# Loading the first tile of a streamed dot product in four strided transfers

## The chip, the cores and the metric

The kernel runs on one core of one Trainium2 chip. The metric is the time of one execution on the device, in microseconds (us); lower is better. Times below are medians of several executions. Executions in the normal (fast) state lie within 1 us of their kernel's median, most of them within 0.4; the few executions in a slower state are named where they occur and are not used in comparisons. The span in a profile (first to last instruction) is some 1.8 us shorter than the time of the same execution.

## The reference

x is 8 x 2048 x 4096 float32, 268 MB, and w has 4096 numbers. Each row of x is multiplied with w; along each of the 8 sequences the running maximum of these dot products is taken; a position counts as a record where it reaches that maximum; the output is the running count of records.

```
proj = (x @ w).squeeze(-1)
cm = np.maximum.accumulate(proj, axis=1)
is_record = (proj >= cm).astype(np.float32)
return np.cumsum(is_record, axis=1).astype(np.float32)
```

All the bytes are in x, and each is used once.

## The kernel before

x streams from HBM (the chip's main memory) into three large buffers in SBUF (the memory on the core, 128 rows called partitions). A tile is one sequence's 512 positions: 128 partitions, each with r = 4 neighbouring positions, that is 64 KB per partition and 8 MB in all. (The last group has r = 3, and 128 positions at the end of each sequence are loaded in smaller pieces.) All loads of x are issued by the sync engine's queue in one long list; a load waits only until its buffer is free.

```
for g in range(NG):
    r = RS[g]
    for t in range(B):
        i = SY.dma_start(
            out=at(g, t)[:, : r * D],
            in_=x[B - 1 - t, STARTS[g] : STARTS[g] + r * P, :].rearrange(
                "(p r) d -> p (r d)", r=r
            ),
        ).then_inc(xs[t], 16)
        u, n = user_before(g, t)
        if n:
            i._wait_ge(*(free(u, n)))
        ...
```

The compute of a tile starts when the whole tile has landed: the vector engine (DVE) takes 2816 of the 4096 columns of each row as a fused dot product, the POOL engine multiplies the other 1280, and ACT sums POOL's products. Both wait on the tile's semaphore:

```
def group_dots(r, g=0):
    for t in range(B):
        b, xb = B - 1 - t, at(g, t)
        for j in range(r):
            i = dot(xb[:, j * D : j * D + VC], w_v[:, :VC], ...)
            if j == 0:
                i._wait_ge(xs[t], 16)
        i.then_inc(fr[t], 1)
...
def group_products(r, g=0):
    ...
            i = G.tensor_mul(out=xl, in0=xl, in1=w_sb).then_inc(pl, 1)
            if j == 0:
                i._wait_ge(xs[t], 16)
```

After each group the tensor engine transposes the sums and the vector engine scans them. w is spread to all partitions at the start, beside the load of the first tile.

Of the kernel before, what the change touches and what calls it, by code (L numbers as in the profile page):

```python
# [20 lines left out]
def kernel(  # L21
# [16 lines left out]
    P = 128  # L38
    B, S, D = x.shape
# [8 lines left out]
    STARTS = [sum(RS[:g]) * P for g in range(NG)]  # L48
# [19 lines left out]
    def rows_of(m):  # L68
        return m * H % B, m * H // B * Q
# [41 lines left out]
    def sem(name):  # L111
        return tc.alloc_semaphore(f"{name}_{next(ns)}")
# [1 line left out]
    xs = [sem("xs") for _ in range(B)]  # L114
    fr = [sem("fr") for _ in range(B)]
    xq = [sem("xq") for _ in TILES]
    ws, bw, wc, cs, od, oe, psr, pd, pl, go, sd, pa, con, fo, ms, p7, mg, pg, ml = (
        sem(n) for n in "ws bw wc cs od oe psr pd pl go sd pa con fo ms p7 mg pg ml".split()
    )

    V, A, G, T, SY = nc.vector, nc.scalar, nc.gpsimd, nc.tensor, nc.sync
# [28 lines left out]
    def at(g, t):  # L150
        return xbuf[(t if g < NL else t + NS - 1) % NS]

    def user_before(g, t):
        if t >= NS:
            return t - NS, g + 1
        if g == NL:
            return B - NS + t, g
        return max(u for u in range(B) if u % NS == t), g

    def free(u, n):  # L160
        return (p7, n) if u == B - 1 else (fr[u], 2 * n)

    with tc.tile_critical(no_gpsimd_drain=True):

        for g in range(NG):
            r = RS[g]
            for t in range(B):
                i = SY.dma_start(
                    out=at(g, t)[:, : r * D],
                    in_=x[B - 1 - t, STARTS[g] : STARTS[g] + r * P, :].rearrange(  # L170
                        "(p r) d -> p (r d)", r=r
                    ),
                ).then_inc(xs[t], 16)
                u, n = user_before(g, t)
                if n:
                    i._wait_ge(*(free(u, n)))
                if g == t == 0:
                    A.dma_start(
                        out=w_row, in_=w.rearrange("(k c) one -> k (c one)", k=NW)
                    ).then_inc(ws, 16)  # L180
                if t == 4 and g:
                    SY.dma_start(
                        out=out[:, STARTS[g - 1] : STARTS[g]], in_=cnt
                    )._wait_ge(cs, g + 1).then_inc(od, 16)
# [9 lines left out]
        for i, (m, c0, c1, _, _) in enumerate(TILES):  # L194
            u, xb = slot(m)
            d = SY.dma_start(  # L196
                out=xb[:, c0:c1],
                in_=x[
                    rows_of(m)[0] : rows_of(m)[0] + H,
                    S0 + rows_of(m)[1] : S0 + rows_of(m)[1] + Q, c0:c1,  # L200
                ].rearrange("b i d -> i b d"),
            ).then_inc(xq[i], 16)
# [7 lines left out]
            out=identity, in_=identity, compare_op=ALU.not_equal, fill=1.0,  # L210
# [10 lines left out]
        for n, k in enumerate(order):  # L221
# [3 lines left out]
                out=dst, lhsT=identity[:NW, k : k + 1].to_broadcast([NW, P]),  # L225
# [13 lines left out]
            out=by_b, in_=identity.rearrange("p (i b) -> p b i", b=H),  # L239
# [3 lines left out]
            out=by_i, in_=identity.rearrange("p (i b) -> p i b", b=H), op=ALU.add,  # L243
# [4 lines left out]
        def group_scans(r=R):  # L248
            n = r * P
            scans(cm[:, :n], cnt[:, :n], ps[:B, :n], cm[:, N - 1 :], cnt[:, N - 1 :])  # L250
# [5 lines that stand above are left out]
                    i = dot(  # L256
                        xb[:, j * D : j * D + VC], w_v[:, :VC],
                        sum_v[:, j * B + b : j * B + b + 1],
                    )
                    if j == 0:  # L260
                        i._wait_ge(xs[t], 16)
                i.then_inc(fr[t], 1)

        with V.Fori(0, NL):
            group_scans()
            V.sem_inc(psr, -3)
            group_dots(R)
# [4 lines left out]
# [3 lines that stand above are left out]
                    xl = at(g, t)[:, j * D + VC : (j + 1) * D]  # L275
                    i = G.tensor_mul(out=xl, in0=xl, in1=w_sb).then_inc(pl, 1)  # L276
                    if j == 0:
                        i._wait_ge(xs[t], 16)

        G.wait_ge(wc, 3)  # L280
        with G.Fori(0, NL):
            group_products(R)
# [87 lines left out]
        for m in range(B - 2):  # L370
            k = m // 2
            v, p = acc_v[:, m : m + 1], acc_p[:, m : m + 1]
# [16 lines left out]
        for i in range(B - 2, len(TILES)):  # L389
            n = i - (B - 2)  # L390
            m, p = TILES[i][0], TILES[i][4]
            z = m - (B - 2)
            v, dp = part_v[:, n : n + 1], part_p[:, n : n + 1]
# [53 lines left out]
```

## Time and profile before

| | before |
|---|---|
| time, median of the first 3 runs | 630.17 us |
| span of the profiled run | 629.3 us |
| x by the stream's rate, 268.44 MB at 433 GB/s | 620 us |
| first dot product on x | 22.80 us |

The page's DMA rows and the rates by stretch are in the prediction. Two more views matter for what follows. The first is the rate in the two halves of the first tile's load (columns as in the prediction: start:end, length, five engines, clock, DMA share, GB/s; a packet counts in the stretch where it starts, so short stretches are rough and a DMA share can exceed 1):

```profile
2.00:12.00 10.00, 9.38 (x11) 3.81 (x12) 0.57 (x2) 1.87 (x2) 0.00 (x0) 1.00 1.01 413
12.00:22.00 10.00, 4.63 (x6) 1.33 (x4) 3.58 (x4) 1.47 (x2) 0.00 (x0) 1.00 1.00 433
```

The second is the start of the first dot product in the vector engine's timeline (start us, duration, what, the idle time before it and what ended that):

```profile
22.80 3.09 DVE L124 CUSTOM_DVE_ANT_0 xall<-xall,w_v 128x2816 f32<-128x2816 f32 x1 [0.67 <-DMA xall<-in_x_dram]
```

The first tile streams at once at nearly the full rate, and the vector engine finishes its setup only 0.67 us before the tile is there.

Below, "row" means the data of one partition of a tile, which the trace records as one DMA packet of 65,536 bytes. The records have no engine and no address. In order of their start they fall into rounds of 16, because 16 streams run side by side; each stream is taken to be one DMA engine, which so moves eight rows of a tile. "Row one" is the first such round.

### The profile page before, as it was taken

The numbers are of one execution on the slowest core, as the hardware profiler recorded it, in microseconds if no ns is written. First come the engines' busy times: TensorE is split into PE (matmuls) and PEld (weight loads), VectorE is DVE, ScalarE is ACT, GpSimd is POOL, SyncE is SP. The second block draws the span as 40 slices with busy tenths as digits, with TensorE's granted clock in tenths as the row PEclk, the third lists the DMA queues.
The fourth block names the chain that finished last, engine by engine and source line by source line (L and its number), as shares of the span: only waits on it lengthen the run. The fifth ranks groups of instructions, "written<-read, shape, count | busy, mean of one in ns | idle before, by whom it ended". The sixth has DMA issues, their size and how long they took to land. (4 is left out here: it accounts for less than half of the span.)

```text
span 629.3 us, 1140 instructions
## 1 busy us (share of the span) xinstructions
PE 29.1 (5%) x96; PEld 13.5 (2%) x96; DVE 407.3 (65%) x294; ACT 181.2 (29%) x274; POOL 370.7 (59%) x149
## 2 busy tenths in 40 slices
PE   8000000000020000000001000000002000000100
PEld 3000000000010000000000000000001000000000
DVE  0755775556766567755578655676556976655897
ACT  1222332223322233222233222332223232232254
POOL 0554675456765557745577555676557666555775
PEclk9999999999999999999996555555555555555565
DMA  9999999999999999999999999999999999999996
GB/s 401 400 467 400 446 421 425 442 437 429 442 425 450 417 450 417 459 408 458 408 458 408 458 408 458 408 459 408 462 418 438 416 447 441 413 447 444 404 425 248
DMA packets 6563, 268.54 MB, mean 427 GB/s; under 512 B 760, under 2 KB 1016, under 8 KB 1568
## 3 DMA queue, kind: packets, MB, share of 16 engines
q1 hardware_dynamic: 6544, 268.50, 98.9%
q10 hardware_dynamic: 16, 0.02, 0.0%
q14 instruction: 3, 0.02, 0.0%
HBM read 268.45 MB, written 0.07 MB: 427 GB/s over the span
## 5 line engine op out<-in xcount | busy, mean ns | idle before, releaser
L124 DVE CUSTOM_DVE_ANT_0 xall<-xall,w_v 128x2816 f32<-128x2816 f32 (+1 forms) x129 | 385.5, 3041 | 181.8 <-DMA xall<-in_x_dram 181.8
L276 POOL TENSOR_TENSOR xall<-xall,w_sb 128x1280 f32<-128x1280 f32 x120 | 345.0, 2909 | 246.7 <-DMA xall<-in_x_dram 243.3
L130 ACT ACTIVATE xall<-xall 128x1280 f32<-128x1280 f32 (+2 forms) x130 | 162.9, 1253 | 428.6 <-POOL xall L276 408.3
L312 PE MATMUL ps<-identity,small 128*8 128x128 f32 x60 | 13.0, 406 | 568.6 <-PEq L309 568.6
L130 ACT ACTIVATION_READ_ACCUMULATOR xall<-xall 128x1 f32 x130 | 24.2, 186 | 0.0
L336 POOL TENSOR_TENSOR xall<-xall,w_sb 128x1280 f32<-128x1280 f32 (+2 forms) x8 | 21.1, 2632 | 3.1 <-DMA xall<-in_x_dram 3.0
L312 PEld LDWEIGHTS ps<-identity,small 128*8 128x8 f32 x60 | 7.3, 125 | 575.4 <-issue 571.3
L140 DVE TENSOR_TENSOR_SCAN cm<-ps,cm,small 8x512 f32<-8x512 f32 (+3 forms) x8 | 7.0, 869 | 18.8 <-PE ps L312 18.4
L224 PE MATMUL w_v<-w,identity 8*128 8x512 f32 x14 | 12.1, 1056 | 0.0
L124 DVE DVE_READ_ACCUMULATOR2_ANT small<- 128x1 f32 x133 | 10.8, 81 | 0.0
L246 DVE MEMSET ps<- 8x512 f32 x1 | 0.5, 485 | 15.7 <-ACT w L235 15.7
L146 DVE TENSOR_TENSOR_SCAN cnt<-ps,cnt,small 8x512 f32<-8x512 f32 (+3 forms) x8 | 7.0, 870 | 0.3
L224 PEld LDWEIGHTS w_v<-w,identity 8*128 8x128 f32 x14 | 4.6, 332 | 7.3 <-issue 7.3
L143 DVE TENSOR_TENSOR ps<-ps,cm 8x512 f32<-8x512 f32 (+3 forms) x8 | 3.9, 487 | 0.3
L232 ACT COPY w_sb<-w_v 128x768 f32<-128x768 f32 x1 | 0.8, 799 | 11.4 <-PE w_v L224 11.4
L347 POOL TENSOR_TENSOR masked<-fold,small 128x4 f32<-128x4 f32 x8 | 1.6, 201 | 3.2 <-DVE small L124 3.2
L124 DVE CUSTOM_DVE_ANT_0 xall<-xall,w_v,small 128x480 f32<-128x480 f32 (+2 forms) x4 | 3.1, 810 | 0.2 <-DVE small L124 0.2
L357 PE MATMUL ps<-fold,masked 128*8 128x32 f32 x20 | 2.0, 235 | 25.3 <-ACT masked L352 17.7
L352 ACT ACTIVATE masked<-fold,small 128x4 f32<-128x4 f32 x10 | 3.0, 298 | 0.3
L336 POOL TENSOR_TENSOR xall<-xall,w 128x640 f32<-128x640 f32 (+1 forms) x2 | 2.3, 1137 | 0.1
L224 PE MATMUL ps<-w,identity 8*128 8x512 f32 x2 | 2.1, 1135 | 2.6 <-DMA w<-in_w_dram 2.6
L231 ACT ACT_TABLE_LOAD x1 | 1.3, 1283 | 2.7 <-DVE fold L242 2.7
(18 smaller groups left out, 5.3 us busy)
## 6 DMA issues: line engine op xcount, KB each, us to landing
xall<-in_x_dram SPq DMA_DIRECT2D x8, 6144.0 KB, 33.5
xall<-in_x_dram SPq DMA_DIRECT2D x6, 2048.0 KB, 42.4
xall<-in_x_dram SPq DMA_DIRECT2D x1, 1264.0 KB, 36.6
xall<-in_x_dram SPq DMA_DIRECT2D x1, 816.0 KB, 39.3
xall<-in_x_dram SPq DMA_DIRECT2D x1, 784.0 KB, 37.9
xall<-in_x_dram SPq DMA_DIRECT2D x2, 240.0 KB, 26.6
xall<-in_x_dram SPq DMA_DIRECT2D x1, 416.0 KB, 39.4
xall<-in_x_dram SPq DMA_DIRECT2D x24, 45.0
```

The lines of the kernel that those rows point to most:

```text
L124: return V.tensor_tensor_reduce(out=xsl, in0=xsl, in1=wsl, scale=1.0, scalar=seed, op0=ALU.mult, op1=ALU.add, accum_out=dst,)
L130: return A.activation(out=xsl, in_=xsl, func=ACTF.Copy, accum_out=dst)
L140: V.tensor_tensor_scan(out=cm_, data0=src, data1=low, initial=cm0, op0=ALU.max, op1=ALU.max,)._wait_ge(psr, base).then_inc(psr, 1)
L143: V.tensor_tensor(out=src, in0=src, in1=cm_, op=ALU.is_ge)._wait_ge(psr, base + 1).then_inc(psr, 1)
L146: V.tensor_tensor_scan(out=cnt_, data0=src, data1=low, initial=cnt0, op0=ALU.add, op1=ALU.max,)._wait_ge(psr, base + 2).then_inc(cs, 1)
L224: i = T.matmul(out=dst, lhsT=identity[:NW, k : k + 1].to_broadcast([NW, P]), rhs=w_row, start=True, stop=True,).then_inc(bw, 1)
L276: i = G.tensor_mul(out=xl, in0=xl, in1=w_sb).then_inc(pl, 1)
L312: i = T.matmul(out=ps[:B, j : r * P : r], lhsT=l[:, j * B : (j + 1) * B], rhs=identity, start=k == 0, stop=k == 1,)
L336: G.tensor_mul(out=xl, in0=xl, in1=w_pool(*p))._wait_ge(xq[i], 16).then_inc(pl, 1)
L347: return eng.tensor_tensor(out=e, in0=by_b, in1=acc.to_broadcast([P, H]), op=ALU.mult)
L352: return A.activation(out=e, in_=by_b, func=ACTF.Copy, scale=acc)._wait_ge(pa, na).then_inc(ms, 1)
L357: return T.matmul(out=ps[:B, k * Q : (k + 1) * Q], lhsT=masked[:, n * B : (n + 1) * B], rhs=by_i, start=start, stop=stop,)
```

## The change

The first tile alone is loaded in four transfers of strided partitions instead of one. A new semaphore counts the first three, and both consumers wait for it once. The apparent intent is to give each DMA engine its first row sooner: a first transfer of 16 rows has one for each engine.

```
+                src = x[B - 1 - t, STARTS[g] : STARTS[g] + r * P, :].rearrange(
+                    "(p r) d -> p (r d)", r=r
+                )
+                p0, dp = 0, 1
+                if g == t == 0:
+                    for p0, dp in ((0, 8), (4, 8), (2, 4)):
+                        SY.dma_start(
+                            out=at(g, t)[p0::dp, : r * D], in_=src[p0::dp]
+                        ).then_inc(xf, 16)
+                    p0, dp = 1, 2
                 i = SY.dma_start(
-                    out=at(g, t)[:, : r * D],
-                    in_=x[B - 1 - t, STARTS[g] : STARTS[g] + r * P, :].rearrange(
-                        "(p r) d -> p (r d)", r=r
-                    ),
+                    out=at(g, t)[p0::dp, : r * D], in_=src[p0::dp]
                 ).then_inc(xs[t], 16)
...
+        V.wait_ge(xf, 48)
         with V.Fori(0, NL):
             group_scans()
...
+        G.wait_ge(xf, 48)
         G.wait_ge(wc, 3)
```

More of the change, by code (lines that the diff above doesn't have):

```diff
@@ L116 @@
     xq = [sem("xq") for _ in TILES]
-    ws, bw, wc, cs, od, oe, psr, pd, pl, go, sd, pa, con, fo, ms, p7, mg, pg, ml = (
-        sem(n) for n in "ws bw wc cs od oe psr pd pl go sd pa con fo ms p7 mg pg ml".split()
+    ws, bw, wc, cs, od, oe, psr, pd, pl, go, sd, pa, con, fo, ms, p7, mg, pg, ml, xf = (
+        sem(n) for n in "ws bw wc cs od oe psr pd pl go sd pa con fo ms p7 mg pg ml xf".split()
     )
```

## The prediction

Rival 1: estimates from the measured 2.42 us a row; a "collision" makes a row take twice that, 4.84 us, in parts one and two (630.2 + 4.8 = 635.0) or in all eight rows (630.2 + 19.4 = 649.6).

> **What bounds the kernel now.** I read the page's DMA rows first, then the engine groups, then the rates by stretch, then the issues of the loads, then the trace's records of single DMA packets. The page:
>
> ```profile
> DMA  9999999999999999999999999999999999999996
> GB/s 401 400 467 400 446 421 425 442 437 429 442 425 450 417 450 417 459 408 458 408 458 408 458 408 458 408 459 408 462 418 438 416 447 441 413 447 444 404 425 248
> DMA packets 6563, 268.54 MB, mean 427 GB/s; under 512 B 760, under 2 KB 1016, under 8 KB 1568
> ...
> L124 DVE CUSTOM_DVE_ANT_0 xall<-xall,w_v 128x2816 f32<-128x2816 f32 (+1 forms) x129 | 385.5, 3041 | 181.8 <-DMA xall<-in_x_dram 181.8
> L276 POOL TENSOR_TENSOR xall<-xall,w_sb 128x1280 f32<-128x1280 f32 x120 | 345.0, 2909 | 246.7 <-DMA xall<-in_x_dram 243.3
> ```
>
> The 16 DMA engines are over 90% busy in every slice but the last (the first row). x is 268 MB and nothing of it is read twice. The vector engine's dot products, the busiest compute, take 385.5 us and sit idle 181.8 us, all of it waiting for x. So the span is the time of the stream plus what stands before its first byte and after its last. By stretches (start:end, length, busy time and count of five engines, clock, DMA share, GB/s):
>
> ```profile
> 0.00:2.00 2.00, 0.00 (x0) 0.00 (x0) 0.00 (x0) 0.00 (x0) 1.12 (x11) 1.00 0.12 41
> 0.00:22.00 22.00, 14.01 (x16) 5.14 (x16) 4.15 (x6) 3.34 (x4) 1.12 (x11) 1.00 0.93 388
> 22.00:600.00 578.00, 13.04 (x60) 7.29 (x60) 379.09 (x253) 165.22 (x243) 350.68 (x123) 0.78 1.00 433
> 624.00:629.30 5.30, 0.87 (x8) 0.41 (x8) 1.90 (x8) 0.85 (x4) 0.20 (x1) 0.50 0.02 3
> ```
>
> Two microseconds of start with almost no data, then DMA share 1.00 at 433 GB/s, then a tail of 5 us. The packet records give the unit: a row of the big tiles is one packet of 65,536 bytes, median 2.418 us, that is 27.1 GB/s on one engine, and 16 x 27.1 = 434 GB/s. Each engine moves 268.44 MB / 16 = 16.78 MB, which at 27.1 GB/s takes 619.1 us. First packets start at 1.98 to 2.60 us, last packets end at about 623.7: 621.7 us for 619.1 of work, so about 2.6 us is lost to the staggered start and to slower packets. The first packet of each engine takes 3.06 us on average (2.60 to 3.27), 0.64 over the usual one; from the second row on the first tile runs at 2.418.[...]
>
> **Slack ahead of the stream.** The big loads and the start queue:
>
> ```profile
> L168 SPq DMA_DIRECT2D xall<-in_x_dram x32: 327/328/432, 1.0 to 551.5; - x32
> ...
> DMA to landing us min/median/max: 21.8/44.0/60.1
> ...
> SPq L168 <- ACT xall L130: 52.4, 2, 33.4
> ```
>
> An issue costs the queue about 0.33 to 0.43 us; the first tile lands 21.8 us after it is issued at 1.0; the later ones take a median of 44 us because each stands behind one or two tiles of 19.4 us (8 rows x 2.418). The last line is the queue's waits in the first 60 us: it waits for a buffer, not for its own issuing. Because the stream never runs dry, any time lost in the first tile moves every later row by the same amount and reaches the end undiminished; any time won does too.
>
> [...]
>
> **The change, part by part.**
> - *Removed*: one issue of 128 rows. *Added*: four issues of 16, 16, 32 and 64 rows of the same tile. Bytes, packet size (64 KB a row) and rows per engine (1 + 1 + 2 + 4 = 8, as before, if each part is spread over 16 engines) stay. So the 619.1 us of data stay.
> - *Issuing*: three more issues at 0.43 us = 1.3 us on the queue. Part one is issued at 0.97 as before; parts two to four at about 1.4, 1.9 and 2.3; the second tile moves from 1.43 to about 2.8. From issue to first packet was 1.0 us (0.97 to 1.98), so part two is ready at about 2.4, while no engine ends its first row before 4.9; the second tile is needed at 21.9. Nothing runs dry: cost 0.
> - *Completion packets*: three more 4-byte packets of 9 ns on each engine, 0.03 us. At the boundary of tiles one and two the trace has the next row starting at 21.89 where the last ended at 21.89. Cost 0 to 0.03 us.
> - *New waits*: the vector engine and the POOL engine wait once for the first three parts. These are four rows of eight, there by about 12.8 us (where row four ends now). The vector engine gets there after 18.3 us, held by the w preparation, and both wait for the last part at 22.8 anyway. Cost 0.
> - *Moved*: the order of rows within the tile. The dots start only when all are in, so no gain from early parts. Only the start can differ: the engines now start over 0.62 us (1.98 to 2.60).[...] The slowest engine ends its first row at 5.53. If every engine began at 1.98 and took the same mean of 3.06, that would be 5.04: a gain of 0.5 us. Were the start loss gone too (2.42), 4.40: 1.1 us, the outer bound, 0.2%. I expect 0 to 0.3, since the late starters are those with the quicker first packets[...].
>
> Sum: 630.2 + 0.03 - (0 to 0.3) + 0: about 630.1 if nothing collides.
>
> **Rivals.**
> 1. [...]a row takes 4.84 us in place of 2.42. For parts one and two alone: 2 x 2.42 = +4.8 us, 635.0. [...]every row of the tile collides: 8 x 2.42 = +19.4 us, 649.6, which is 3.1% slower.[...] Against: the last-row tiles, whose source is a 32 x 4 pattern, run all 768 packets of 16 KB at 0.611 us without a single slow one; and the eight 2 KB rows of w, on partitions 0 to 7[...] came in 0.22 us, 74 GB/s[...]. Neither settles it[...].
> 2. *Engine chosen by partition.* Then part one uses eight engines with two rows each and part two the other eight, which start one issue later (0.45 us): +0.2 to +0.5 us, 630.5.
> 3. *The start is really quicker*: 0.3 to 1.1 us won, 629.1 to 629.9. For it, the 0.62 us stagger; against, that the first packets are slow together.
> 4. *Hidden anyway*: rows are reordered and nothing is seen, 630.2 within the 0.35 us that the three runs differ.
>
> **Range and chances.** I give 60% to rivals 3 and 4 and the plain sum (629.5 to 630.4), 18% to rival 2 (630.3 to 630.8), 12% to a part collision (632 to 637), 10% to a collision in the whole tile. Most of this is within 1 us of the time before; I put the point at 630.3, a little up for the tail of collisions, and choose the range 629.6 to 635.5, which leaves mostly the full collision outside. 2% is 12.6 us: no gain of that size exists in the start (outer bound 1.1 us), so faster 0.01; slower needs the full collision, 0.1; same 0.89.
>
> **What would show it.** In the changed kernel: the page's GB/s in the first two slices still near 400[...]; the first dot on x still starting near 22.8 us; 64 KB packets of rows two to eight of the first tile at 2.418 us (4.8 means rival 1); the starts of first packets closer than 0.62 us (my reading of the stagger) or in two groups 0.45 apart (rival 2); the DVE and POOL waits for the three parts at nothing; the rate 22 to 600 us unchanged at 433 GB/s; the tail of 5 us unchanged. I am wrong if the first tile lands more than 1 us off 22.8, or if the later rate moves, which nothing above foresees.

## The result, and the profile after

The changed kernel takes 635.32 us (635.07 to 635.38, 4 runs) against 630.34 (630.15 to 630.57, 4 runs) before: 5.0 us more. The ratio is 1.0078, with a 95% interval of 1.0061 to 1.0096. Here and below a ratio is the mean time of one kernel's fast runs over that of the other's in the same rounds, so it is not quite the ratio of the quoted medians. The result is correct. The page:

```profile
DMA  9999999999999999999999999999999999999995
GB/s 266 397 463 414 447 451 410 456 405 459 401 459 430 434 451 410 456 405 459 401 459 434 430 455 405 455 407 459 401 437 441 444 441 407 445 444 444 402 427 240
...
L124 DVE CUSTOM_DVE_ANT_0 xall<-xall,w_v 128x2816 f32<-128x2816 f32 (+1 forms) x129 | 385.5, 3041 | 186.1 <-DMA xall<-in_x_dram 186.1
```

Against the rows that the prediction shows, one number stands out: the first slice moved 266 GB/s, not 401. The DMA row still shows 9 there: the engines were busy, but slow. The dots themselves cost the same 385.5 us; the vector engine's wait for x grew from 181.8 to 186.1. The stretches at the start, and the long one that follows:

```profile
2.00:12.00 10.00, 9.44 (x11) 3.81 (x12) 0.57 (x2) 1.87 (x2) 0.00 (x0) 1.00 1.04 229
12.00:22.00 10.00, 4.58 (x6) 1.33 (x4) 3.64 (x4) 1.47 (x2) 0.00 (x0) 1.00 0.96 400
...
22.00:600.00 578.00, 10.69 (x50) 6.07 (x51) 374.72 (x251) 163.56 (x240) 346.96 (x121) 0.78 1.00 434
```

Most of the loss lies before 12 us, where 229 GB/s stand for 413 before, with the DMA share unchanged at about 1; from 12 to 22 us it is still 400 for 433. After 22 us the stream runs at 434, as it did. The first dot and the queue's issues of the three new transfers (duration in ns as minimum/median/maximum, first and last start):

```profile
27.99 3.09 DVE L124 CUSTOM_DVE_ANT_0 xall<-xall,w_v 128x2816 f32<-128x2816 f32 x1 [5.92 <-DMA xall<-in_x_dram]
```

```profile
L174 SPq DMA_DIRECT2D xall<-in_x_dram x3: 569/592/612, 1.0 to 2.2; - x3
...
DMA to landing us min/median/max: 7.8/12.0/16.1
```

The first dot is 5.2 us later. These issues take 0.59 us each, where the whole first tile's took 0.40; the trace has 0.61 for the second tile's too, which is loaded whole as before, so the stride is not what makes an issue long. Part one, whose rows should land about 3 us after they start, lands 7.8 us after its issue. The packet records give the sum (means over the 16 streams, worked out from the records of both traces; no view prints them):

| step of the first tile | before | after | difference, us |
|---|---|---|---|
| start of row one | 2.19 | 2.55 | +0.35 |
| row one takes | 3.06 | 4.85 (part one) | +1.79 |
| row two | 2.42 | 4.90 (part two) | +2.49 |
| row three | 2.42 | 2.89 (part three) | +0.47 |
| rows four to eight, each | 2.42 | 2.42 | 0 |
| next tile's first row starts | 22.16 | 27.28 | +5.12 |

The four differences add up to 5.1, and the next tile starts 5.1 us later. From there on nothing is won or lost. The profiled spans differ by only 4.3 us because the profiled run of the kernel before was a little slow itself: 197 of its 64 KB packets after 20 us were over 2.43 us, against 2 in the changed kernel's, which cost it 1.1 us per engine; its own time was 631.05, about 0.9 above its median.

### The profile page after: what moved, and what is told of

Read it like the earlier page. It is cut to its first block, busy times and chain, and to the rows that moved or that the text cites. A ratio compares the mean times of both kernels' runs of the same rounds, so it can differ in the third digit from the quotient of the medians.

```text
span 633.6 us, 1144 instructions
## 1 busy us (share of the span) xinstructions
PE 29.2 (5%) x96; PEld 13.6 (2%) x96; DVE 407.2 (64%) x294; ACT 181.2 (29%) x274; POOL 370.6 (58%) x149
## 5 line engine op out<-in xcount | busy, mean ns | idle before, releaser
L124 DVE CUSTOM_DVE_ANT_0 xall<-xall,w_v 128x2816 f32<-128x2816 f32 (+1 forms) x129 | 385.5, 3041 | 186.1 <-DMA xall<-in_x_dram 186.1
```

The costliest lines, as they stand in the source:

```text
L124: return V.tensor_tensor_reduce(out=xsl, in0=xsl, in1=wsl, scale=1.0, scalar=seed, op0=ALU.mult, op1=ALU.add, accum_out=dst,)
```

## The experiments

**Theory.** The loss comes from where the rows go: rows that run side by side into certain partitions slow one another. The assumption was a factor of two for every 8th partition and for 64 neighbours, four for 16 neighbours, two or four for 32, and none for every 2nd or every 4th partition; each of these is measured below. What the rows would share no view of the traces shows. In each expectation the theory's forecast is the first one given.

**Rivals.** (a) Each further transfer costs something by itself. (b) The rows read side by side in HBM are 512 KB apart in parts one and two, a large power of two, and that is slow. (c) The loss belongs to the start of the stream. (d) Transfers of few rows are slow because of the row count.

All edits below are made to the changed kernel.

### Four transfers of every 4th partition

```
-                    for p0, dp in ((0, 8), (4, 8), (2, 4)):
+                    for p0, dp in ((0, 4), (2, 4), (1, 4)):
...
-                    p0, dp = 1, 2
+                    p0, dp = 3, 4
```

> Four transfers as in the change, but each of 32 partitions (every 4th from 0, 2, 1 and 3)[...]. [...]630.3 us, +-0.4, like the kernel before, and the first tile's rows two to eight take 2.418 us. Cost-per-transfer theory (each further transfer costs its issue, its completion or its wait some 1.7 us): again about 635.3. Row-pitch theory (16 engines reading rows 512 KB apart in HBM are slow): 630.3 too, as the rows read together lie closer[...].

Measured: 630.74 us (5 runs) against 630.45 before (9 runs in the same rounds), ratio 1.0004, interval 0.9991 to 1.0018. The rows take 3.10, 2.42, 2.42 us and so on. The stretches:

```profile
2.00:12.00 10.00, 9.37 (x11) 3.83 (x12) 0.57 (x2) 1.87 (x2) 0.00 (x0) 1.00 1.04 419
12.00:22.00 10.00, 4.65 (x6) 1.33 (x4) 3.57 (x4) 1.47 (x2) 0.00 (x0) 1.00 0.97 419
```

The rate is back at once. As many transfers, waits and semaphores as in the change cost nothing like 5 us, so rival (a) falls. What is left shows in the trace, not clearly in the times: row one starts at 2.48 us on average against 2.19, after a first issue of 0.57 us against 0.40.

### The same destinations, with the reads close together

```
-                    for p0, dp in ((0, 8), (4, 8), (2, 4)):
+                    for p0, dp, rows in (
+                        (0, 8, src[0:64:4]), (4, 8, src[64:128:4]), (2, 4, src[2::4]),
+                    ):
                         SY.dma_start(
-                            out=at(g, t)[p0::dp, : r * D], in_=src[p0::dp]
+                            out=at(g, t)[p0::dp, : r * D], in_=rows
```

> The change as it is, but parts one and two read their rows 256 KB apart[...]; their destinations stay on every 8th partition. Wrong result on purpose (wrong rows for one batch). [...]no change from the changed kernel, 635.3, the first two rows of each engine 4.85 and 4.90 us. Row-pitch theory: back to about 630.3, these rows at 3.06 and 2.42 us.

Measured: 635.04 us (4 runs), ratio 1.0073 (1.0057 to 1.0088). Rows one and two take 4.67 and 4.94 us, row three 2.85. The result is wrong in one sequence, which has no bearing on the time. The stretches:

```profile
2.00:12.00 10.00, 9.41 (x11) 3.82 (x12) 0.57 (x2) 1.87 (x2) 0.00 (x0) 1.00 1.06 242
12.00:22.00 10.00, 4.61 (x6) 1.33 (x4) 3.61 (x4) 1.47 (x2) 0.00 (x0) 1.00 0.92 387
```

Source rows 256 KB apart do not help: the destinations alone keep the loss.

### The far reads, into every 4th partition

```
-                    for p0, dp in ((0, 8), (4, 8), (2, 4)):
+                    far = x[B - 1].rearrange("(p r) d -> p (r d)", r=32)[:32, : r * D]
+                    for p0, dp, rows in ((0, 4, far), (2, 4, src[2::4])):
                         SY.dma_start(
-                            out=at(g, t)[p0::dp, : r * D], in_=src[p0::dp]
+                            out=at(g, t)[p0::dp, : r * D], in_=rows
...
-        V.wait_ge(xf, 48)
+        V.wait_ge(xf, 32)
```

(and the same for POOL's wait)

> First part to every 4th partition from 0 (32 rows[...]), but its source rows 512 KB apart in HBM, like those of part one and two of the change; then every 4th from 2, then the odd ones as in the change. Wrong result on purpose. [...]630.3, rows of the first part at about 3.1 and 2.42 us. Row-pitch theory: the two rows of each engine in the first part near 4.9 us, 635 in all.

Measured: 630.51 us (4 runs), ratio 1.0002 (0.9986 to 1.0017); rows one and two at 3.19 and 2.42 us. Wrong result again.

```profile
2.00:12.00 10.00, 9.44 (x11) 3.82 (x12) 0.57 (x2) 1.87 (x2) 0.00 (x0) 1.00 1.05 419
12.00:22.00 10.00, 4.58 (x6) 1.33 (x4) 3.64 (x4) 1.47 (x2) 0.00 (x0) 1.00 0.97 419
```

With the run before this settles rival (b): 64 KB rows read 512 KB apart (or at multiples of it: which of the 32 run side by side is not recorded) come at full speed, and the loss follows the destination. Only these two experiments part the source from the destination; in those below the rows that are read change with the partitions.

### All eight rows into every 8th partition

```
-                    for p0, dp in ((0, 8), (4, 8), (2, 4)):
+                    for p0, dp in [(k, 8) for k in (0, 4, 2, 6, 1, 5, 3)]:
...
-                    p0, dp = 1, 2
+                    p0, dp = 7, 8
...
-        V.wait_ge(xf, 48)
+        V.wait_ge(xf, 112)
```

> The first tile in eight transfers of every 8th partition. [...]all eight rows of each engine take about 4.85 us in place of 2.42; from the kernel before that is +0.4 for the later start, +1.8 for row one and 7 x 2.48 = 17.4, in all about +19.5: 649.8. Theory that only the start of the stream is slow (the first two rows, whatever follows): 635.5. Cost per transfer, 1.7 us each: 7 x 1.7 = +12: 642.

Measured: 649.95 us (4 runs), ratio 1.0309 (1.0294 to 1.0325), within 0.2 us of what the theory said. All eight rows are slow: 4.79 us, then 4.89 to 4.91. Its stretches, which before stood at 413 and 433 GB/s:

```profile
2.00:12.00 10.00, 9.40 (x11) 3.82 (x12) 0.57 (x2) 1.87 (x2) 0.00 (x0) 1.00 1.09 236
12.00:22.00 10.00, 4.61 (x6) 1.33 (x4) 0.48 (x1) 1.47 (x2) 0.00 (x0) 1.00 1.10 236
```

The loss grows with the number of rows that each engine moves to every 8th partition (two: +5.0 us, eight: +19.5), not with the start of the stream, so rival (c) falls, and (a) again, as that had asked for 642.

### Sixteen neighbours

```
-                    for p0, dp in ((0, 8), (4, 8), (2, 4)):
+                    for p0 in range(0, P - 16, 16):
                         SY.dma_start(
-                            out=at(g, t)[p0::dp, : r * D], in_=src[p0::dp]
+                            out=at(g, t)[p0 : p0 + 16, : r * D], in_=src[p0 : p0 + 16]
...
-                    p0, dp = 1, 2
+                    p0, dp = P - 16, 1
```

(with the waits at 112)

> The first tile in eight transfers of 16 neighbouring partitions each. [...]every row takes four times 2.42 = 9.67 us, the tile 77 in place of 19.4 us, about +58: 688. A theory by which eight colliding pairs share something between the engines, whatever the partition, and 16-row transfers are slow as such: rows at 4.85 us, 650. Row-pitch theory (rows 64 KB apart): 630.

Measured: 684.6 us in the three fast runs (684.48 to 684.69; a fourth, at 783.8, was slow), ratio 1.0858 (1.0838 to 1.0878). Row one takes 8.60 us, the others 9.23 to 9.24.

```profile
2.00:12.00 10.00, 9.40 (x11) 3.82 (x12) 0.57 (x2) 1.87 (x2) 0.00 (x1) 1.00 1.63 190
12.00:22.00 10.00, 4.62 (x6) 1.33 (x4) 0.48 (x1) 1.47 (x2) 0.00 (x0) 1.00 0.93 105
```

The row count is the same as in the run before, but into neighbours the rows take nearly twice as long (9.24 us against 4.89). So the row count alone does not set the time, against rival (d); the two halves below settle it. The time was 3.4 us under the 688 expected: a row took 3.8 times the usual 2.42 us, not four times. Also seen here: eight issues take 0.40 to 0.46 us each, and row one starts at 2.14 us on average against 2.19 before. So the later start after the change does not come from the number of transfers.

### Thirty-two neighbours

```
-                    for p0, dp in ((0, 8), (4, 8), (2, 4)):
+                    for p0 in range(0, P - 32, 32):
```

(and the slices, last start and waits accordingly)

> The first tile in four transfers of 32 neighbouring partitions[...]. Tells how 32 rows are dealt to 16 engines. [...]rows at 9.67 us, the tile 77: 688. [...]the tile 38.7 us: 650; in the last case only eight streams run at 2.42 us a row, in the former 16 at 4.84.

Two outcomes: 688, and 650, the latter with 16 streams at 4.84 us a row or with eight at 2.42. The trace does not record which engine a row is dealt to.

Measured: 651.0 us in the four fast runs (two slow ones at 720.3 and 722.6), ratio 1.0326 (1.031 to 1.0341).

> The four transfers of 32 neighbouring partitions again, since their first profile fell in the slow state. [...]16 streams, rows of 4.89 us, 651.0 in a fast run. A rate of 5.12 us as in the slow profile would mean that the slow state did not touch the first tile.

Measured: 650.98 us (2 runs), ratio 1.0327 (1.0306 to 1.0347). There are 16 streams; row one takes 4.80 us, the others 4.91 to 5.13. So rows into 32 neighbours take twice the 2.42 us of rows into every 4th partition, in transfers of as many rows. Why 32 neighbours are slow by two and 16 by nearly four the runs do not show: the trace has no engine and no address. The 5.12 us of the slow profile came close to the 5.13 of the fast one; rows of the later tiles took 2.71 us in it against 2.42. Three of the twelve runs with 16 or 32 neighbours were slow and no other run was; whether that has to do with these kernels stays open.

### Two halves: near and alternate

```
near:  for p0 in range(0, P - 64, 64): ... [p0 : p0 + 64] ...; last part from P - 64
alternate:  for p0, dp in ((0, 2),): ...; last part p0, dp = 1, 2
```

(waits at 16 in both)

> The first tile in two transfers, partitions 0 to 63 and then 64 to 127. [...]all eight rows of each engine take 4.89 us, as in the eight transfers of every 8th partition, less the later start of strided issues: 649.6. Theory that 16-row and 32-row transfers are slow for their row count: 630.3.

> The first tile in two transfers, the even and then the odd partitions[...]. [...]630.7, as the four transfers of every 4th partition, that is the kernel before plus about 0.3 for the longer issue of a strided transfer. Theory that splitting in halves costs by itself: like the near halves.

Measured: 651.44 us for the near halves (ratio 1.0334, 1.0316 to 1.0351) and 630.78 for the alternate ones (1.0008, 0.9991 to 1.0024), 4 runs each. Rows take 4.94 to 5.13 us in the former and 3.11, then 2.42 in the latter. First the near, then the alternate halves:

```profile
2.00:12.00 10.00, 9.40 (x11) 3.82 (x12) 0.57 (x2) 1.87 (x2) 0.00 (x0) 1.00 1.01 210
12.00:22.00 10.00, 4.62 (x6) 1.33 (x4) 0.48 (x1) 1.47 (x2) 0.00 (x0) 1.00 1.03 210
```

```profile
2.00:12.00 10.00, 9.43 (x11) 3.81 (x12) 0.57 (x2) 1.87 (x2) 0.00 (x0) 1.00 1.04 419
12.00:22.00 10.00, 4.59 (x6) 1.33 (x4) 3.63 (x4) 1.47 (x2) 0.00 (x0) 1.00 0.97 419
```

Two transfers of 64 rows, the same bytes, a factor of two in rate: only which partitions a transfer holds differs, and with them the rows it reads. So rival (d) falls. The near halves came out 1.8 us above what was expected: some 1.5 because neighbours take up to 5.13 us a row where every 8th partition takes 4.89, which stays open, and the rest because row one starts late here too, at 2.54 us. The expectation had put the late start down to the stride, and the near halves have none, yet their issue is as long:

```profile
L174 SPq DMA_DIRECT2D xall<-in_x_dram x1: 578/578/578, 1.0 to 1.0; - x1
```

In all the traces row one starts at 2.14 to 2.34 us on average where the first issue took 0.39 to 0.40 us, and at 2.48 to 2.61 where it took 0.56 to 0.61. What makes an issue long, neither the stride nor the number of transfers explains; it stays open.

### The change in the middle of the stream

```
-                if g == t == 0:
+                if g == NL and t == 0:
+                    SY.wait_ge(*free(*user_before(g, t)))
...
+        V.wait_ge(xf, 48)
         group_dots(RS[-1], NL)
```

(POOL likewise; the waits at the start are gone)

> The change moved from the very first tile to the first tile of the last group (48 KB rows, 384 KB apart in part one), in the middle of the stream; the first tile as before. [...]two rows of each engine take twice 1.815 us, so 2 x 1.8 = +3.6: 633.9. Theory that the loss belongs to the start of the stream: 630.3. Row-pitch theory (a power of two needed): 630.3.

Measured: 634.43 us (5 runs) against 630.33 (9 runs), ratio 1.0063 (1.005 to 1.0077). The rows of 48 KB, 1.815 us each before, take 3.25, 3.58, 2.55 and 1.93 us and then 1.82: together 4.05 us more, and the time is 4.1 us longer. The stretch from 466 to 476 us, first of the kernel before, then of this one:

```profile
466.00:476.00 10.00, 0.00 (x0) 0.00 (x0) 7.09 (x5) 2.61 (x4) 7.05 (x3) 0.50 0.92 400
```

```profile
466.00:476.00 10.00, 0.00 (x0) 0.00 (x0) 6.21 (x5) 1.74 (x3) 6.16 (x3) 1.00 1.02 265
```

The loss is not one of the start, and the stream, being the bound, hands it to the end in full. Expected were 3.6 us; as in the change itself, the row after the two slow ones is slow too (2.55 us here, 2.89 there).

## Why the prediction was right or wrong

The measured 635.3 us lies at the upper edge of the range, and "within 2%" held. But the point, 630.3, stood on the wrong branch: what happened is the first rival, rows of parts one and two at about twice the usual time, which had been given 12%. That the range held is partly luck: its upper end of 635.5 lies 0.2 us above the measured time.

- **The bound** was right: the stream sets the time, compute waits, and time lost in the first tile reaches the end undiminished. A delay of 5.1 us in the first tile became 5.0 us in the time.
- **The failed step** is the choice between "if nothing collides" and rival 1. The prediction gave 60% to nothing colliding; what the runs showed is rows one and two at 4.85 and 4.90 us in place of 3.06 and 2.42. The rival's size was right in sum, in part by luck: +4.8 us estimated for parts one and two, +4.75 measured in rows one to three. The estimate had it as 2 x 2.42; row one lost only 1.79, since its usual 3.06 is already 0.64 over 2.42, and row three lost 0.47 that the estimate lacked. The row after slow ones is slow elsewhere too, even in an ordinary load of 128 partitions: the second tile's first row took 2.89 us after the eight transfers of every 8th partition and 3.50 after those of 16 neighbours. Why, no run shows. That parts three and four would not collide, the condition for +4.8 and not +19.4, was seen: from row four on the rows take 2.42.
- **The evidence weighed against it** was weak. The last-row tiles at full speed have 128 partitions as their destination, so they say nothing about 16. The 16 KB of w in 0.22 us were a short burst of 2 KB packets, and say little about rows of 64 KB.
- **Issuing at cost 0** was wrong by a little. The issues took 0.57 to 0.61 us, not 0.43, and row one starts 0.35 us later. The three splits into every 2nd or every 4th partition put the whole price of splitting at 0.1 to 0.4 us in their medians, at the limit of what the runs resolve.
- **The stagger** of the engines' starts was misread. With a first part of one row per engine it went from 0.62 to only 0.54 us, and with 16 neighbours as the first part it was 0.62 again; with the first tile whole, in the run with the change in the middle, it was 0.93. So it does not follow the number of rows in the first transfer, and the hoped-for gain of 0 to 0.3 us did not show.
- **Rival 2** (eight engines in part one) is out: part one's 16 rows run side by side, starting from 2.36 to 2.90 us.
- **Completion packets and new waits** cost nothing that can be told, as said: four transfers of every 4th partition stayed at 630.7, and the vector engine and POOL start when the last part lands.

No version tried beats the kernel before. The start can be spoiled by splitting, and nothing here made it quicker.

## What to carry to other kernels

If a kernel is bound by its loads and a load must be split by partitions, split it into every 2nd or every 4th partition, which here kept the usual 2.42 us a row, and not into every 8th (4.89 us) or into blocks of 16, 32 or 64 neighbours (up to 9.24, 5.13 and 5.13 us): here that was the difference between at most +0.4 us and +5 to +54 us for one tile. Busy DMA engines do not prove a healthy stream (here a DMA share of 1.04 at 229 GB/s): look at GB/s, and at the time of single packets against the usual one. In this stream, which never runs dry, a loss at its head was paid in full at its end (5.1 us in the first tile, 5.0 in the time), though the vector engine was idle for 186.1 us.
